# The low half of every third MLP weight chunk by an adding DMA, in a one-core hybrid decoder step

## The chip, the cores and the metric

The kernel runs on one core of a Trainium2 chip. The metric is the time of one execution on the device, in microseconds. The engines that appear below are TensorE (PE; its weight loads are listed as PEld), VectorE (DVE), ScalarE (ACT), GpSimd (POOL) and SyncE (SP), and the DMA queues that SP, ACT and POOL issue to.

## The reference

One layer of a hybrid decoder trunk is computed for 256 prompt tokens and 8 sample tokens, 264 columns in all, with a width of 2048. Three gated branches (pooling, a gated linear recurrence, a Conformer convolution) are merged and projected, and a squared-ReLU MLP follows. Everything is float32. Cut to what matters here:

```python
x = x + (g_a * y_pool + g_b * y_lru + g_c * y_conf) @ w_out
hid = jnp.square(jax.nn.relu(rms_norm(x, g_mlp) @ w_up))   # w_up   (2048, 8192)
x = x + hid @ w_down                                       # w_down (8192, 2048)
...
y_prompt = rms_norm(xp, g_final)
```

## The kernel before, in words

Activations are kept transposed, features on the 128 partitions and the 264 tokens along the row. TensorE multiplies in the rounded format float32r, and a float32 product is made of three: both operands are written as a high half (the value rounded) plus a low half (the value less its rounding), and `mm3` (lines 183 to 187) adds high times high (L185), high times low (L186) and low times high (L187) into one accumulator.

All weights come as one stream. `weight_plan` cuts it into groups, and each group into chunks of 128 rows by 1024 numbers (512 KB); a chunk of a dense group holds two blocks of 128 input rows by 512 output columns, and so feeds 2 x 4 x 3 = 24 products. The order of the groups in the MLP is, for each quarter q of the 8192 hidden features: four groups of the up projection, `("w_up", 0, 16, q*4+m)`, then four of the down projection, `("w_down", q*16, 16, m)`, eight chunks each. So a quarter is 64 chunks, and the two halves of a quarter 32 each.

A chunk passes through three buffers. SP's DMA brings chunks in pairs (1 MB, `dma_pair`, L138) into `raw`, which has six slots. `split` (lines 156 to 163) makes its two halves: ACT casts the raw chunk to the high half in `whi` (L162), and DVE subtracts that from the raw chunk into `wlo` (L163). `whi` and `wlo` have four slots each. Then PE multiplies.

The order of every engine's work is the order of the calls, written out by hand in one loop over the chunks. In step i of the loop come, in this order: the split of chunk i+3; in even steps, the DMA of chunks i+8 and i+9; the products of chunk i; after the last chunk of a group, what takes its four accumulators away; and the background work that falls due, taken from small queues by a budget for each engine. The waits between engines follow from the buffers: the split of chunk i+3 writes the slots of `whi` and `wlo` that chunk i-1 used, and the DMA of chunks i+8 and i+9 writes the slots of `raw` that chunks i+2 and i+3 used.

For a tile of the up projection the accumulator is clipped and scaled by DVE (L806), squared and cast by ACT (L810, L811), and its low half taken by DVE (L815), a step or two later. For a tile of the down projection DVE adds the accumulator to the residual (L830), and in the last quarter ACT squares it and POOL sums the squares (L796). Otherwise POOL has no work in the MLP, and it issues no DMA anywhere in the kernel. The program sets aside 1024 bytes of each partition for descriptors of POOL's DMAs (`dynamic_dma_scratch_size=1024`).

Of the kernel before, what the change touches and what calls it, by code (L numbers as in the profile page):

```python
# [12 lines left out]
AF = mybir.ActivationFunctionType  # L13
ALU = mybir.AluOpType
# [37 lines left out]
EARLY = 2  # L52
WIDE = 4
ROW = N + CH


def weight_plan():

    groups = [("w_lru_in", 0, 2 * WIDE, 0)] + [("w_in", WIDE, KD - WIDE, m) for m in (1, 2)]
    groups += [("w_in", 0, 16, m) for m in (0, 3, 4, 6, 5)]
    for g in range(4):
        groups += [("w_gate", 0, 16, t) for t in ((0, 4, 1), (5,), (2, 6), (3, 7))[g]]
        groups += [("w_pool_br", 0, 4, g), ("w_lru_br", 0, 8, g)]
    groups += [("w_gate", 0, 16, 8 + g) for g in range(3)]
    groups += [("w_conf_br", 0, 4, 0), ("w_gate", 0, 16, 11)]
    groups += [("w_conf_br", 0, 4, g) for g in range(1, 4)]
    groups += [("w_out", 0, 16, m) for m in range(4)]
    for q in range(4):  # L70
        groups += [("w_up", 0, 16, q * 4 + m) for m in range(4)]
        groups += [("w_down", q * 16, 16, m) for m in range(4)]
    chunks = []
    for gi, (name, _, k, m) in enumerate(groups):
        for c in range(k // 2):
            chunks.append(("wide" if name == "w_lru_in" else "dense", gi, c, CH))
            if name == "w_in" and (m, c) in LRU_AT:
                chunks.append(("lru", LRU_AT.index((m, c)), 0, 512))
            if (name, m) == ("w_gate", 0) and c == 3:
                chunks += [("grp", 0, 0, 512), ("none", 0, 0, 0)]  # L80
    return groups, chunks
# [3 lines left out]
def hybrid_step(ctx: ExitStack, tc: tile.TileContext, head_in, x_in, par_in, st_in, wall, y_out, st_out):  # L85
    nc = tc.nc
# [4 lines left out]
    def f(ap):  # L91
        return ap.bitcast(F32)
# [5 lines left out]
    qtmp = cpool.tile([P, 16 * N], F32, name="qtmp", tag="Q")  # L98
    first = cpool.tile([P, KD + EARLY * ROW], F32, name="first")
    early = first[:, KD:].rearrange("p (k c) -> p k c", k=EARLY)  # L100
# [29 lines left out]
    groups, chunks = weight_plan()  # L130
# [25 lines left out]
    def split(j, a=0, b=CH):  # L156
        if j >= len(chunks) or not chunks[j][3]:
            return
        h, lo = whi[:, j % NHI, :], wlo[:, j % NHI, :]
        s = slice(a, min(b, chunks[j][3]))  # L160
        r = early[:, j, N + s.start:N + s.stop] if j < EARLY else raw[:, j % NRAW, s]
        nc.scalar.copy(h[:, s], r)  # L162
        nc.vector.tensor_tensor(lo[:, s], r, f(h[:, s]), op=ALU.subtract)  # L163

    def sent(x):
# [125 lines left out]

    cuts = [0, KD + N + 256, KD + ROW, KD + ROW + N + 512, KD + 2 * ROW]
    for a, b in zip(cuts, cuts[1:]):
# [614 lines left out]
    for a in range(0, CH, 256):  # L908
        split(0, a, a + 256)
    for c in (1, 2):  # L910
        x_tile(c)
        split(c, 0, 512)
        split(c, 512, CH)
# [198 lines left out]
```

## Time and profile before

| | |
|---|---|
| measured time, median of two runs | 1300.28 us (1300.14 to 1300.42) |
| span of the profiled execution, first to last instruction | 1299.3 us |
| TensorE busy | 1287.7 us, 99% of the span |
| DVE busy | 834.7 us, 64% |
| ACT busy | 717.7 us, 55% |
| POOL busy | 104.6 us, 8% |
| moved by DMA | 256.96 MB, 198 GB/s over the span |
| share of the 16 DMA engines' time, SP's queue | 57.8% |

The profiled execution's own span stands 1.0 us below the median of the measured runs. Busy times are sums over one execution. An engine's row in a list of groups gives the line, the operation, what it writes and reads, the count, the total and the mean, and then how long the engine sat idle just before these instructions and what ended that. Rows in order of time begin with the start, in microseconds from the first instruction, and the length. A row of 40 numbers cuts its window into 40 equal slices.

### The profile page before, as it was taken

The numbers are of one execution on the slowest core, as the hardware profiler recorded it, in microseconds if no ns is written. First come the engines' busy times: TensorE is split into PE (matmuls) and PEld (weight loads), VectorE is DVE, ScalarE is ACT, GpSimd is POOL, SyncE is SP. The second block draws the span as 40 slices with busy tenths as digits, with TensorE's granted clock in tenths as the row PEclk, the third lists the DMA queues.
The fourth block names the chain that finished last, engine by engine and source line by source line (L and its number), as shares of the span: only waits on it lengthen the run. The fifth ranks groups of instructions, "written<-read, shape, count | busy, mean of one in ns | idle before, by whom it ended". The sixth has DMA issues, their size and how long they took to land.

```text
span 1299.3 us, 26672 instructions
## 1 busy us (share of the span) xinstructions
PE 1287.7 (99%) x11434; PEld 1286.8 (99%) x11434; DVE 834.7 (64%) x1058; ACT 717.7 (55%) x1021; POOL 104.6 (8%) x124
## 2 busy tenths in 40 slices
PE   9999999999999999999999999999999999999996
PEld 9999999999999999999999999999999999999996
DVE  6896898776776677666655555655555555555554
ACT  7767677667674655455544334543344533354543
POOL 0250010110102023021000000000000000000013
PEclk9999999999999999999999999999999999999998
DMA  8656566555565564656555555555555555555551
GB/s 337 220 186 202 191 207 200 195 195 198 196 229 193 186 206 161 232 185 206 195 194 198 195 197 194 198 197 194 197 195 196 195 197 195 197 196 196 195 195 68
DMA packets 38711, 256.96 MB, mean 198 GB/s; under 512 B 4288, under 2 KB 5312, under 8 KB 9152
## 3 DMA queue, kind: packets, MB, share of 16 engines
q1 hardware_dynamic: 38304, 254.78, 57.8%
q8 instruction: 89, 1.46, 0.4%
q10 hardware_dynamic: 288, 0.47, 0.1%
q14 instruction: 30, 0.25, 0.1%
HBM read 252.03 MB, written 3.21 MB: 196 GB/s over the span
## 4 chain that ended last, share of the span: by engine, by line
PE 99%; DVE 0%; DMA 0%; ACT 0%; SPq 0%; DVEq 0%; issue 0%
PE acc L187 33%; PE acc L186 33%; PE acc L185 33%; PE acc L894 1%; DMA first<-head_dram 0%; DVE raw L999 0%; PE acc L980 0%; SPq L151 0%; DVE acc L993 0%; DVEq L1091 0%; DVE G L992 0%; DVE G L991 0%; ACT whi L162 0%; ACT A L284 0%; PE acc L259 0%
## 5 line engine op out<-in xcount | busy, mean ns | idle before, releaser
L163 DVE TENSOR_TENSOR wlo<-raw,whi 128x1024 fp32r<-128x1024 f32 (+1 forms) x479 | 585.6, 1225 | 442.1 <-ACT whi L162 436.5
L162 ACT CAST whi<-raw 128x1024 fp32r<-128x1024 f32 (+1 forms) x479 | 493.6, 1033 | 526.1 <-PE acc L186 474.7
L187 PE MATMUL acc<-A,wlo 128*128 128x264 f32 x1952 | 538.9, 276 | 0.0
L186 PE MATMUL acc<-A,whi 128*128 128x264 f32 x1952 | 538.8, 276 | 0.0
L185 PE MATMUL acc<-A,whi 128*128 128x264 f32 x1952 | 538.7, 276 | 0.0
L187 PEld LDWEIGHTS acc<-A,wlo 128*128 128x128 f32 x1952 | 368.9, 189 | 0.1
L185 PEld LDWEIGHTS acc<-A,whi 128*128 128x128 f32 x1952 | 368.9, 189 | 0.0
L186 PEld LDWEIGHTS acc<-A,whi 128*128 128x128 f32 x1952 | 368.9, 189 | 0.0
L186 PE MATMUL acc<-xn,whi 128*128 128x264 f32 x1024 | 282.6, 276 | 0.0
L187 PE MATMUL acc<-xn,wlo 128*128 128x264 f32 x1024 | 282.6, 276 | 0.0
L185 PE MATMUL acc<-xn,whi 128*128 128x264 f32 x1024 | 282.6, 276 | 0.0
L185 PEld LDWEIGHTS acc<-xn,whi 128*128 128x128 f32 x1024 | 193.5, 189 | 0.0
L186 PEld LDWEIGHTS acc<-xn,whi 128*128 128x128 f32 x1024 | 193.5, 189 | 0.0
L187 PEld LDWEIGHTS acc<-xn,wlo 128*128 128x128 f32 x1024 | 193.5, 189 | 0.0
L186 PE MATMUL acc<-Q,whi 128*128 128x264 f32 x644 | 177.7, 276 | 0.0
L185 PE MATMUL acc<-LH,whi 128*128 128x264 f32 x640 | 176.6, 276 | 0.0
L187 PE MATMUL acc<-LH,wlo 128*128 128x264 f32 x640 | 176.6, 276 | 0.0
L186 PEld LDWEIGHTS acc<-Q,whi 128*128 128x128 f32 x644 | 121.7, 189 | 0.0
L185 PEld LDWEIGHTS acc<-LH,whi 128*128 128x128 f32 x640 | 121.0, 189 | 0.0
L187 PEld LDWEIGHTS acc<-LH,wlo 128*128 128x128 f32 x640 | 121.0, 189 | 0.0
L796 POOL TENSOR_TENSOR G<-G 128x264 f32<-128x264 f32 x28 | 25.5, 911 | 745.3 <-ACT G L794 744.4
L576 ACT ACTIVATE G<-tmp,par 128x256 f32<-128x256 f32 x120 | 54.2, 499 | 2.9 <-DVE G L579 2.0
(186 smaller groups left out, 797.3 us busy)
## 6 DMA issues: line engine op xcount, KB each, us to landing
raw<-wall_dram SPq DMA_DIRECT2D x230, 1024.0 KB, 4.9
raw<-wall_dram SPq DMA_DIRECT2D x10, 512.0 KB, 7.0
raw<-wall_dram SPq DMA_DIRECT2D x5, 256.0 KB, 3.0
X<-x_dram SPq DMA_DIRECT2D x4, 264.0 KB, 8.5
so_dram<-st SPq DMA_DIRECT2D x1, 1018.0 KB, 9.1
st<-st_dram SPq DMA_DIRECT2D x1, 912.0 KB, 9.8
y_dram<-raw SPq DMA_DIRECT2D x4, 198.0 KB, 2.2
X<-x_dram SPq DMA_DIRECT2D x1, 528.0 KB, 9.9
```

The costliest lines, as they stand in the source:

```text
L162: nc.scalar.copy(h[:, s], r)
L163: nc.vector.tensor_tensor(lo[:, s], r, f(h[:, s]), op=ALU.subtract)
L185: nc.tensor.matmul(ps[:, :N], whi_t, xh, start=first, stop=False)
L186: nc.tensor.matmul(ps[:, :N], whi_t, xl, start=False, stop=False)
L187: nc.tensor.matmul(ps[:, :N], wlo_t, xh, start=False, stop=last)
L576: nc.scalar.activation(dst[:, ct, :TP], vext[:, ct, k:k + TP], AF.Copy, scale=par[:, w:w + 1])
L796: nc.gpsimd.tensor_tensor(sq2, sq2, t, op=ALU.add)
L894: nc.tensor.matmul(pair[m][:, :N], w[:, m * P:(m + 1) * P], sent(A[:, x, :]), start=start and k == 0, stop=False)
```

## The change

For chunks of the up projection and of two of the four quarters of the down projection (the second and third, whose first rows are blocks 16 and 32), and of those only the chunks whose index in the stream divides by three, the low half is made in another way. ACT, after its cast, writes the negated rounding of the raw chunk to the low half's slot. POOL then issues a DMA from `raw` to that slot which adds what it brings to what stands there. The value is the same: minus the rounding, plus the raw weight. DVE's subtraction is not issued for these chunks. Of the stream's 478 chunks 192 are in the named groups (indices 222 to 253 and 286 to 445), and 64 of these divide by three.

```diff
+LOW_BY_DMA = (("w_up", 0), ("w_down", 16), ("w_down", 32))
...
         nc.scalar.copy(h[:, s], r)
+        if chunks[j][0] == "dense" and groups[chunks[j][1]][:2] in LOW_BY_DMA and j % 3 == 0:
+            nc.scalar.activation(lo[:, s], r, AF.Copy, scale=-1.0)
+            nc.gpsimd.dma_start(lo[:, s], r, accum_op=ALU.add)
+            return
         nc.vector.tensor_tensor(lo[:, s], r, f(h[:, s]), op=ALU.subtract)
```

## The prediction

> **What bounds the kernel now.** I read the page first (busy shares, then the chain that ended last), then the busy time of the stretches that the change touches, then one period of the weight pipeline in order of time, and last the DMA rows. The page:
>
> ```profile
> span 1299.3 us, 26672 instructions
> PE 1287.7 (99%) x11434; PEld 1286.8 (99%) x11434; DVE 834.7 (64%) x1058; ACT 717.7 (55%) x1021; POOL 104.6 (8%) x124
> PE 99%; DVE 0%; DMA 0%; ACT 0%; SPq 0%; DVEq 0%; issue 0%
> ```
>
> TensorE is the whole chain. The up and down projections fill the last 690 us; by the plan's order the groups that the diff names lie in two stretches, the up projection of the first quarter (595.8 to 682.2) and then everything from the second up projection to the fourth (768.6 to 1200.6). In these two and the one between them:
>
> ```profile
> core 0: us, PE busy (x) PEld busy (x) DVE busy (x) ACT busy (x) POOL busy (x), PEclk, DMA share, GB/s
> 595.80:682.20 86.40, 86.40 (x770) 86.40 (x769) 53.28 (x71) 47.91 (x69) 3.31 (x4) 1.00 0.58 194
> 682.20:768.60 86.40, 86.40 (x770) 86.40 (x769) 46.04 (x53) 36.41 (x40) 0.00 (x0) 1.00 0.59 196
> 768.60:1200.60 432.00, 432.00 (x3842) 432.00 (x3841) 238.47 (x285) 199.77 (x248) 0.00 (x0) 1.00 0.58 195
> ```
>
> PE is busy for every microsecond of them at full clock. DVE stands at 55% and ACT at 46% of the long stretch, so work taken from DVE there buys no time: **the best this change can do is nothing**. The stretches hold 32 and 160 chunks, 2.70 us each (432.00/160); every index divisible by three makes 64 chunks (43 of the up, 21 of the down projection). The question is only whether the new low half comes in time. One period, in order of time:
>
> ```profile
> 819.75 0.33 SPq L138 DMA_DIRECT2D raw<-wall_dram  x1
> ...
> 820.03 0.28 PE L185 MATMUL acc<-xn,whi 128*128 128x264 f32 x1
> ...
> 820.12 1.04 ACT L162 CAST whi<-raw 128x1024 fp32r<-128x1024 f32 x1 [1.65 <-PE acc L186]
> ...
> 820.15 0.19 PEld L187 LDWEIGHTS acc<-xn,wlo 128*128 128x128 f32 x1
> ```
>
> ```profile
> 821.20 1.23 DVE L163 TENSOR_TENSOR wlo<-raw,whi 128x1024 fp32r<-128x1024 f32 x1 [0.78 <-ACT whi L162]
> ...
> 822.73 0.28 PE L185 MATMUL acc<-xn,whi 128*128 128x264 f32 x1
> ...
> 828.13 0.28 PE L185 MATMUL acc<-xn,whi 128*128 128x264 f32 x1
> ...
> 828.25 0.19 PEld L187 LDWEIGHTS acc<-xn,wlo 128*128 128x128 f32 x1
> ```
>
> At 820.03 PE starts step i. That frees the buffer of chunk i-1, and with four buffers this is the one for chunk i+3. ACT's cast starts 0.09 later, released by PE; DVE writes the low half until 822.43. PE starts step i+3 three periods later, at 828.13, and loads its first low weights at 828.25. Counted from the step's start, the low half is there at 2.40 and wanted at 8.22: today 5.8 us lie idle in between. **That slack is all the change has to live on.**
>
> **What is removed.** 64 of DVE's subtractions, 64 x 1.226 = 78.5 us of DVE time:
>
> ```profile
> L163 DVE TENSOR_TENSOR wlo<-raw,whi 128x1024 fp32r<-128x1024 f32 x160 | 196.2, 1226 | 193.5 <-ACT whi L162 191.2
> L162 ACT CAST whi<-raw 128x1024 fp32r<-128x1024 f32 x160 | 167.3, 1046 | 230.8 <-PE acc L186 228.3
> ```
>
> DVE waits for ACT in front of nearly every one of them. Worth on the path: 0.
>
> **What is added on ACT.** A second pass over the chunk (the negated rounding), same shape and engine as the cast: 64 x 1.046 = 66.9 us. It follows the cast at once, so the next thing of ACT is 1.05 us later in one step of three. ACT idles 1.65 us ahead of its casts, which covers it; only beside the squares of the up projection (about two steps in eight) is ACT full, and there the next cast is late by at most that 1.05 us, with 5.8 us of slack behind it. Cost 0. The new pass ends at 0.09 + 2 x 1.08 = 2.25 after the step's start (1.08 is from the cast's start, 820.12, to what it releases, 821.20).
>
> **What is added on POOL.** 64 DMAs, each from raw into the low half, adding. They wait for ACT. Behind them on POOL stands nothing: the long stretch has 0.00 us of POOL work, and only its last quarter's sums of squares come later. From 2.25 the transfer has 5.97 us to land.
>
> **What the transfer costs.** No POOL DMA and no adding one is in the trace. The nearest rows are the weight loads of twice its size, one of them in a window of 6 us (its 40 slices are 0.15 us each), and the stores of y at the end (a window from 1287, slices of 0.325 us):
>
> ```profile
> L138 SPq DMA_DIRECT2D raw<-wall_dram x124: 327/328/328, 599.6 to 1262.6; - x124
> DMA to landing us min/median/max: 4.6/4.9/5.8
> ```
>
> ```profile
> DMA  0000000000000098702268799979797979724000
> raw<-wall_dram SPq DMA_DIRECT2D x1, 1024.0 KB, 4.8
> ```
>
> ```profile
> 771.15 16.53 SPq L138 DMA_DIRECT2D raw<-wall_dram  x4
> ```
>
> ```profile
> GB/s 0 0 0 0 0 0 0 0 0 0 0 0 0 175 385 375 366 336 336 406 380 392 240 377 357 397 383 395 380 445 408 122 24 0 0 0 0 0 0 0
> y_dram<-raw SPq DMA_DIRECT2D x2, 264.0 KB, 2.8
> ```
>
> The load issued at 771.15 has its first bytes moving at about 772.1 (0.95 us), its last at 775.5, and has landed at 775.95 (0.45). Its engine time is the share: 0.58 x 5.40 us a pair = 3.13 us for 1 MB. Stores that leave SBUF run near 385 GB/s, 2.7 us for 1 MB. The adding transfer writes 0.5 MB and reads 1 MB (raw, and the low half itself). **Lower end**, as if it were a plain copy of 0.5 MB: 1.57 us of engine time. **Upper end**: there is no row for the adder's rate; I bound it by twice the 2.7 us of 1 MB, 5.4. I take 2.7, both operands counted at the rate of the row that leaves SBUF, since that is the nearest in kind. For POOL's own part, SP's issue of 0.33 us is the lower bound; I take 0.74, the shortest of POOL's passes over a 128x264 tile:
>
> ```profile
> L796 POOL TENSOR_TENSOR G<-G x28: 742/756/1403, 532.7 to 1285.7; 128x264 f32<-128x264 f32 x28
> ```
>
> Alone, it lands at 2.25 + 0.74 + 0.95 + 2.7 + 0.45 = 7.09, in time by 1.1 us.
>
> The Trainium skill, "Collectives: The Full Stack", on why ReduceScatter is half of AllGather, says that a reducing DMA is slow because of its two source reads on one queue, not because of the adder; no run shown here can tell. By that rule the sum is the one with 2.7, without it the lower end.
>
> **But it isn't alone.** raw has six slots, refilled two at a time by SP, and SP now has to wait for the adding DMA to have read its slot. Today SP issues a pair each 5.4 us, at 2.42 into a step (819.75 against 817.33, the start of the step before 820.03), as DVE releases it:
>
> ```profile
> SPq L138 <- DVE wlo L163: 473.5, 95, 6.4
> ```
>
> Take the six steps from the start of step 6m as 0. The refill behind chunks 6m+2 and 6m+3 waits for the add of chunk 6m+3, 7.1 to 8.1; the refill behind it, whose own release comes at 2 x 2.70 + 2.42 = 7.8, queues right after. So 2 MB of loads go out together at about 7.9, moving from 8.85 to 8.85 + 6.26 = 15.1. The next add (chunk 6m+6) is ready at 8.10 + 2.25 = 10.35 and moving at 10.35 + 0.74 + 0.95 = 12.04, with 3.1 us of loads still to go. If the two share the engines evenly, its 2.7 us take 5.4: moved at 17.44, landed at 17.9. It is wanted at 16.20 + 0.12 = 16.32: **1.6 us late**, and PE stands for it. The third refill goes out only then, so the add after that one (moving 3.9 us after its step starts) meets a load almost finished, and is in time. One add in two is late: 32 x 1.6 = 51 us. The refills themselves are in time: a pair issued at 8.2 and held up to about 16 is first cast at 5 x 2.70 + 0.09 = 13.59 at the earliest for one chunk, and that chunk has the 5.8 us of slack.
>
> **Sum.** Span 1299.3 + 51 = 1350.3. The two measured runs have a median of 1300.28, 1.0 above the span, so 1351. With the add's engine time between 2.2 and 3.4 the lateness goes from 0.6 to 2.7 (at 3.4 the load ends first), so this case runs from 1319 to 1387.
>
> **The rivals.** *All hidden.* The point from which it decides is an add that lands within 5.97 us of its start beside a load in flight. With 1.57 us of engine time and 0.33 of issue it moves from 11.63 to 14.8 and has landed at 15.2, ahead of 16.32: no stall, PE as before, 1300. For it: 42% of the DMA time is idle. Against it: the loads come in bunches, and the second operand has to be read. The Trainium skill, "DMA: Bandwidth & Descriptors", on the anatomy of a DMA issued by GpSimd, gives 2.0 us plus the bytes over 436 GB/s; for 1 MB that is an estimate of 4.4 us, in time here with 1.6 to spare; the load's row, 4.9, is a little above that rule.
>
> *The adder is slow.* At 5.4 us of engine time an add that meets no load lands at 9.8, already 1.6 late, each time: 64 x 1.6 = 102. And six chunks need 9.4 us of loads and 10.8 of adds, 20.2 in 16.2 us: DMA becomes the bound, 32 x 4.0 = 128. With the bunching on top I put it at 150: 1450. It decides from 3.83 us of engine time (5.97 less 0.74, 0.95 and 0.45). For it: an operation of which no row says anything. Against: nothing in the trace.
>
> *Faster.* Only through the end, where the time after PE's last product is DVE's; the diff leaves the last down projection as it is. I give it 0.01.
>
> **How the numbers follow.** One add in two late 0.46, all hidden 0.31, slow adder 0.22, faster 0.01. The predicted time is that of the first, 1351. The range goes from 1299 (hidden) to 1460, which takes in the upper end of the unknown rate and leaves out the worse half of the slow adder; the likeliest case's own range is 1319 to 1387. Two per cent, 26 us, is about what a measurement of this kernel can tell from no change: it is 0.8 us for each late add. Below it lie the hidden case and a tenth of the first: 0.35. Slower: 0.42 + 0.22 = 0.64. Faster: 0.01.
>
> **What would show it.** Right: PE's busy time about 1288 still in a longer span, with idle ahead of products or weight loads of L187 put down to the DMA into wlo, 1 to 3 us, about 30 times, in both stretches and nowhere else; two weight loads landing late (over 6 us) out of every three; L163 at 415 instead of 479; the adding DMA landing near 5 us and near 7.5 us in turn. Wrong: stalls at all 64 (then the rate or POOL's part is the larger term), no idle of PE at all, stalls on the cast of ACT (then the refills of raw are what is late), or a granted clock below 1.00 in these stretches, which today's rows have nowhere there.

## The result, and the profile after

The changed kernel takes 1396.67 us (median of two runs, 1391.26 and 1402.08) against 1300.28: a ratio of 1.074, with a 95% interval of 1.064 to 1.084. It is 96 us slower. The profiled execution has a span of 1389.5 us, 90.2 above the one before, and the numbers below are worked out against that. Five lines are new, so the loads' line 138 has become L139, ACT's cast in line 162 is L163, DVE's subtraction in line 163 is L168, and L185 to L187 are L190 to L192.

The head of the page, its chain, and the groups that are new or changed:

```profile
span 1389.5 us, 26849 instructions
PE 1322.3 (95%) x11434; PEld 1315.6 (95%) x11434; DVE 756.7 (54%) x994; ACT 778.2 (56%) x1085; POOL 160.4 (12%) x188
q0 software_dynamic: 9216, 33.56, 13.0%
PE 81%; DMA 13%; ACT 4%; issue 1%; DVE 1%; DVEq 0%
L168 DVE TENSOR_TENSOR wlo<-raw,whi 128x1024 fp32r<-128x1024 f32 (+1 forms) x415 | 507.1, 1224 | 590.6 <-ACT whi L163 586.9
L166 POOL DMA_DIRECT2D wlo<-raw x64 | 55.7, 871 | 636.5 <-ACT wlo L165 549.7
L165 ACT ACTIVATE wlo<-raw 128x1024 fp32r<-128x1024 f32 x64 | 67.3, 1052 | 0.0
```

DVE lost 78.0 us of work, ACT gained a pass of 67.3, and neither moved the end (a run further down has ACT's pass alone). What did is in the chain: 13% of it is now the adding DMA. The table of waits says how often PE stood for it (total, times, longest), and the answer on line 166 how long the adds took to land:

```profile
PEld acc L192 <- DMA wlo<-raw: 61.7, 30, 4.1
```

```profile
L166 POOL DMA_DIRECT2D wlo<-raw x64: 859/869/1024, 589.3 to 1279.3; - x64
DMA to landing us min/median/max: 4.5/6.7/10.3
```

30 of 64 adds were late, by 2.06 us on the mean. That is 61.7 us, and 28.5 of the 90.2 are left. POOL's own issue took 0.86 to 1.02 us for all 64 adds, late or not, so the lateness does not arise there. PE is *busier* than before by 34.6 us with the same 11434 products. Two stretches right after one of the waits, and the chain across it (start, length, what), show why:

```profile
core 0: us, PE busy (x) PEld busy (x) DVE busy (x) ACT busy (x) POOL busy (x), PEclk, DMA share, GB/s
905.10:908.50 3.40, 3.40 (x18) 3.40 (x17) 0.00 (x0) 0.57 (x1) 0.00 (x0) 0.50 0.76 220
909.00:913.00 4.00, 4.00 (x38) 4.00 (x37) 3.52 (x6) 1.04 (x1) 0.00 (x0) 1.00 0.68 153
```

```profile
895.46 8.44 DMA wlo<-raw
903.95 0.38 PE acc L192
...
905.42 0.22 PE acc L190
905.64 0.22 PE acc L191
905.86 0.22 PE acc L192
...
908.69 0.11 PE acc L190
908.81 0.11 PE acc L191
```

The add landed at 903.9, and about a microsecond later the granted clock fell to 0.50 for 3.4 us: products 0.22 us apart instead of 0.11. The waits divide in two. 15 lasted 2.39 us or more, 48.3 us together, and each of them was followed by such a slow stretch; 15 lasted 1.96 us or less, and none of them was. The 15 stretches at 0.50 are 58.0 us long (13 of 3.41 us, two of 6.83), so half of that, 29 us of work, was lost in them. That is the 28.5 that the waits leave. The row of the whole part of the program with adds agrees: 0.04 of 680 us is 27, where before the change the clock stood at 1.00.

```profile
600.00:1280.00 680.00, 624.22 (x5244) 618.46 (x5242) 253.85 (x333) 334.79 (x407) 54.85 (x64) 0.96 0.76 218
```

So a long wait is paid twice, once as idle time and once as slow products after it; a short one is paid once.

Why an add is late shows in one of them. SP issued two loads in the 0.80 us from 913.40, the second at 913.82, and POOL the add at 916.09. Here are those issues, and who used the DMA engines in the 4.5 us after the add's issue and in the 4 us after that (queue, packets, MB, share of the engines):

```profile
913.40 0.80 SPq L139 DMA_DIRECT2D raw<-wall_dram  x2
```

```profile
916.09 0.86 POOL L166 DMA_DIRECT2D wlo<-raw  x1 [11.67 <-ACT wlo L165]
```

```profile
q1 hardware_dynamic: 194, 1.46, 97.5%
```

```profile
q0 software_dynamic: 144, 0.52, 66.2%
q1 hardware_dynamic: 31, 0.12, 8.7%
```

From 916.1 to 920.6 the engines moved nothing but loads. Then all 144 packets of the add moved within 4 us. It did not share the engines evenly with the loads in front of it: it stood behind them. All 15 of the long waits have this picture, two loads issued together, 0.4 to 3.5 us ahead of the add.

### The profile page after: what moved, and what is told of

The parts are those of the page before. It is cut to its first block, busy times and chain, and to the rows that moved or that the text cites. A ratio compares the mean times of both kernels' runs of the same rounds, so it can differ in the third digit from the quotient of the medians.

```text
span 1389.5 us, 26849 instructions
## 1 busy us (share of the span) xinstructions
PE 1322.3 (95%) x11434; PEld 1315.6 (95%) x11434; DVE 756.7 (54%) x994; ACT 778.2 (56%) x1085; POOL 160.4 (12%) x188
## 3 DMA queue, kind: packets, MB, share of 16 engines
q0 software_dynamic: 9216, 33.56, 13.0%
## 4 chain that ended last, share of the span: by engine, by line
PE 81%; DMA 13%; ACT 4%; issue 1%; DVE 1%; DVEq 0%
PE acc L192 27%; PE acc L191 26%; PE acc L190 26%; DMA wlo<-raw 13%; ACT whi L163 2%; ACT wlo L165 2%; PE acc L899 1%; DVE raw L1004 0%; PE acc L306 0%; DVE wlo L168 0%; ACT xn L782 0%; ACT G L799 0%; PE acc L985 0%; DVE xn L787 0%; DVE acc L998 0%
## 5 line engine op out<-in xcount | busy, mean ns | idle before, releaser
L168 DVE TENSOR_TENSOR wlo<-raw,whi 128x1024 fp32r<-128x1024 f32 (+1 forms) x415 | 507.1, 1224 | 590.6 <-ACT whi L163 586.9
L163 ACT CAST whi<-raw 128x1024 fp32r<-128x1024 f32 (+1 forms) x479 | 493.4, 1033 | 555.7 <-PE acc L191 475.4
L192 PE MATMUL acc<-A,wlo 128*128 128x264 f32 x1952 | 540.8, 277 | 8.8 <-DMA wlo<-raw 8.8
L190 PE MATMUL acc<-A,whi 128*128 128x264 f32 x1952 | 540.3, 277 | 0.0
L192 PEld LDWEIGHTS acc<-A,wlo 128*128 128x128 f32 x1952 | 370.5, 190 | 9.8 <-DMA wlo<-raw 9.8
L190 PEld LDWEIGHTS acc<-A,whi 128*128 128x128 f32 x1952 | 370.5, 190 | 0.0
L192 PE MATMUL acc<-xn,wlo 128*128 128x264 f32 x1024 | 292.9, 286 | 36.3 <-DMA wlo<-raw 36.1
L190 PE MATMUL acc<-xn,whi 128*128 128x264 f32 x1024 | 290.2, 283 | 0.0
L191 PE MATMUL acc<-xn,whi 128*128 128x264 f32 x1024 | 290.1, 283 | 0.0
L192 PEld LDWEIGHTS acc<-xn,wlo 128*128 128x128 f32 x1024 | 201.1, 196 | 40.5 <-DMA wlo<-raw 40.4
L190 PEld LDWEIGHTS acc<-xn,whi 128*128 128x128 f32 x1024 | 201.0, 196 | 0.0
L191 PEld LDWEIGHTS acc<-xn,whi 128*128 128x128 f32 x1024 | 200.9, 196 | 0.0
L192 PE MATMUL acc<-LH,wlo 128*128 128x264 f32 x640 | 180.2, 282 | 10.7 <-DMA wlo<-raw 10.7
L190 PE MATMUL acc<-LH,whi 128*128 128x264 f32 x640 | 179.7, 281 | 0.0
L192 PEld LDWEIGHTS acc<-LH,wlo 128*128 128x128 f32 x640 | 123.9, 194 | 11.5 <-DMA wlo<-raw 11.5
L166 POOL DMA_DIRECT2D wlo<-raw x64 | 55.7, 871 | 636.5 <-ACT wlo L165 549.7
L190 PEld LDWEIGHTS acc<-LH,whi 128*128 128x128 f32 x640 | 124.0, 194 | 0.0
L165 ACT ACTIVATE wlo<-raw 128x1024 fp32r<-128x1024 f32 x64 | 67.3, 1052 | 0.0
```

Of the source, the lines that this page charges most:

```text
L165: nc.scalar.activation(lo[:, s], r, AF.Copy, scale=-1.0)
L166: nc.gpsimd.dma_start(lo[:, s], r, accum_op=ALU.add)
L190: nc.tensor.matmul(ps[:, :N], whi_t, xh, start=first, stop=False)
L191: nc.tensor.matmul(ps[:, :N], whi_t, xl, start=False, stop=False)
L192: nc.tensor.matmul(ps[:, :N], wlo_t, xh, start=False, stop=last)
```

## The experiments

Times below are medians; the kernel before ran on the same chips at 1300.7 to 1300.9. Theory A, from the prediction: adds are late because refills of `raw`, held back by the add before them, go out in pairs and stand in front. Theory B: every add has a price of its own. Theory C: loads and adds meet anyway, held back or not.

**One add in six chunks.** `j % 3 == 0` becomes `j % 6 == 0`.

> Every sixth chunk instead of every third: 32 adds, one in 16.2 us. Theory A (an add is late only when two refills of raw, held back by the add before, stand in front of it): no add is late, 1300 to 1305, every add landing near 4.5 to 5 us, clock 1.00 throughout. Rival B (each add costs PE something by itself, by its latency and POOL's part): half of the loss stays, near 1345.

Measured 1301.42, ratio 1.0007 (0.9998 to 1.0017).

```profile
PEld acc L192 <- DMA wlo<-raw: 1.2, 5, 0.3
```

An add without another one in the six chunks is in time, and costs nothing; B falls. 64 adds cost 96 us, and half of them none.

**The constant block.** The add brings other data of the same size, so nothing holds the refills.

```diff
-            nc.gpsimd.dma_start(lo[:, s], r, accum_op=ALU.add)
+            nc.gpsimd.dma_start(lo[:, s], early[:, 0, N:], accum_op=ALU.add)
```

> The 64 adds bring a constant block (chunk 0's raw weights) instead of the raw chunk, so the refill of raw no longer waits for them; the low halves are then other numbers, the traffic is the same. Theory A, if the held refills are the whole cause: loads go out every 5.4 us again, no add is late, 1300 to 1310. Rival C (adds and loads meet anyway, since in every second add a load is released in the same step): one add in two late by 1.3 to 4 us, 1345 to 1450.

Measured 1448.02, ratio 1.1136 (1.1120 to 1.1153): *slower* than the change by 51 us. The waits of PE, and an add's issue beside the load's:

```profile
PEld acc L192 <- DMA wlo<-first: 91.5, 31, 4.8
```

```profile
1007.07 0.33 SPq L139 DMA_DIRECT2D raw<-wall_dram  x1
```

```profile
1007.45 0.86 POOL L166 DMA_DIRECT2D wlo<-first  x1 [11.56 <-ACT wlo L165]
```

So A falls as the whole cause. Without the tie, the load is released by the same pass of ACT that releases the add, goes out 0.4 us ahead of it, and the add stands behind it: 31 late adds of 2.95 us. The tie had kept at least the add's own refill behind it. This is C, in a sharper form, theory D: **an add waits for every load issued ahead of it, and is late where one went out just before.** "Ahead" counts from the add's first packet, which in the run with one add in six comes 1.4 us after POOL starts its issue, at the soonest. In the change a load issued at 903.96, 0.4 us *after* an add's issue at 903.56, still moved from 904.5 on, and the add only from 907.5.

**The phase.** D says that where the adds fall against the loads decides, with the same traffic. Loads go out in even steps. Indices 0 and 2 modulo six put the splits of all adds into odd steps; 0 and 3 put every second one into an even step. The number of adds in six chunks stays two.

```diff
-... and j % 3 == 0:
+... and j % 6 in (0, 2):
```

With the constant block:

> A constant block is added, as before, so no refill waits for an add; but the adds fall on chunks whose index modulo six is 0 or 2, the same two in six, where before it was 0 and 3. Their splits are then all in odd steps, and loads go out in even ones. Theory D (an add waits for every load issued ahead of it, and is late only where one went out just before): each add is ready at 3.7 us after its step's start, when the load of the step before has just moved; it lands at 6.9 to 7.4 us, ahead of 8.2: 1300 to 1310. Rival (the DMA engines are simply too full with this traffic): about 1448 again.

Measured 1318.15, ratio 1.0139 (1.0116 to 1.0161).

```profile
PEld acc L192 <- DMA wlo<-first: 16.1, 10, 5.0
```

130 us faster than the constant block at 0 and 3, with the same loads and as many adds: the DMA engines are not too full. In 51 of the 54 adds that were in time the nearest load was issued 2.0 to 3.7 us ahead. It is not the 1300 to 1310 that was expected: ten waits are left. Three of them, of 3.6 to 5.0 us, make 12.7 of the 16.1, and D covers one of these three, with a load issued 0.3 us ahead. Before the other two the load went out 2.78 us ahead, as it did for dozens of adds that were in time. In one of them, issued at 959.72, most of the add had moved by 964.5, but its last packets came one by one until 969, beside a load that was issued 2.6 us *behind* it (the two windows are 961 to 964.5 and 964.5 to 969.7):

```profile
q0 software_dynamic: 130, 0.48, 69.5%
q1 hardware_dynamic: 64, 0.40, 37.2%
```

```profile
q1 hardware_dynamic: 135, 0.97, 56.0%
q0 software_dynamic: 14, 0.05, 4.8%
```

So D is not the whole rule: now and then an add's tail is overtaken by a later load. Why is open.

With the raw chunk, so that refills wait again:

> The raw chunk is added, as in the change, for indices 0 and 2 modulo six. The refills wait for the adds again and so move towards the next one: by theory D the second add of each six is some 0.5 us late, 1310 to 1340. If holding the refills is harmless, 1300 to 1305; if the phase doesn't matter, about 1396.

Measured 1402.58, ratio 1.0761 (1.0720 to 1.0803), near the change itself.

```profile
PEld acc L192 <- DMA wlo<-raw: 73.2, 32, 4.4
```

The forecast by D had the sign right and the size wrong: 2.3 us late and not 0.5, and then the clock. The time is rather that of the rival beside it, that the phase doesn't matter (1396). The trace is against that rival, and so is the pair of runs with the constant block: 27 of the 32 late adds here have one load issued within 1.3 us of their own issue (up to 0.6 us after it), where the long waits of the change had two, issued together further ahead. Refills that wait have shifted, so that loads and adds meet again. The four runs together:

| | refills wait for the add | refills free |
|---|---|---|
| indices 0 and 3 of six | 1396.7 (the change) | 1448.0 |
| indices 0 and 2 of six | 1402.6 | 1318.2 |

Neither the phase alone nor the tie alone makes the loss. Three combinations put a load in front of about one add in two (30, 31 and 32 of 64 were late); the fourth doesn't (10).

**A copy in place of the add.** `accum_op=ALU.add` is left out.

> The 64 DMAs of POOL copy raw to the low half and don't add (the low halves are then wrong by that). If the second operand's read is what fills the DMA engines, their time goes from 2.7 us to about 1.4 each, and by my queue of loads and adds none is late: 1300 to 1310. If POOL's part and the waiting behind the loads is what counts, and not the size, the copies land as late as the adds and the loss stays above 60.

Measured 1335.87, ratio 1.0244 (1.0192 to 1.0297). The rows below are of an execution of 1321.28, the least of the four; the other three took 1336 to 1337, so the rows account for 20 of the 35 us, and where the rest goes isn't shown.

```profile
q0 software_dynamic: 9216, 33.56, 7.0%
```

```profile
PEld acc L192 <- DMA wlo<-raw: 17.2, 19, 2.7
```

The page counts the same 33.56 MB, but the engines' time is 7.0% of a span of 1319.5, 1.44 us a transfer, against 13.0% of 1389.5, 2.82 us, for the add. So the adding transfer takes twice the engine time of the copy, as the Trainium skill, "Collectives: The Full Stack", on why ReduceScatter is half of AllGather, has it of a reduce with two source reads; the trace agrees. Both expectations missed: half the size took away two thirds of the loss, not all and not none. A transfer half as long still stands behind the loads: ahead of 18 of these 19 waits stand two loads, issued within 2.0 to 4.1 us before the copy.

**The adds to one side.** They go to a block nobody reads; DVE makes the low half.

```diff
             nc.scalar.activation(lo[:, s], r, AF.Copy, scale=-1.0)
-            nc.gpsimd.dma_start(lo[:, s], r, accum_op=ALU.add)
-            return
+            nc.gpsimd.dma_start(early[:, j % 2, N:], r, accum_op=ALU.add)
```

> The 64 adds go to a block that nobody reads, and DVE makes the low half as before (after ACT's pass). The refills of raw still wait for the adds. Theory A: PE waits for nothing, though loads go out in bunches and some land late: 1300 to 1305. Rival: late refills of raw hold up ACT's casts and cost by themselves, 1310 to 1340.

Measured 1300.83, ratio 1.0000 (0.9991 to 1.0010). The traffic, and refills held by the adds, cost nothing. Only PE's wait for the low half does.

**ACT's pass alone.** The same without any DMA of POOL.

> ACT's negated pass alone, 64 times, and then DVE's subtraction over it as before; no DMA of POOL. Prediction's step: ACT's time is covered, 1300 to 1302. Rival: ACT's 1.05 us in one step of three delays casts where ACT is full, up to 1310.

Measured 1300.97, ratio 1.0001 (0.9992 to 1.0010). The pass is covered.

**As many adds, spread out.** `j % 4 == 0` over all up and down projections.

> 64 adds again, but every fourth chunk, over all up and down projections. Theory A: an add lands before the two refills behind it meet the next add, six chunks' bunch doesn't build up: 1300 to 1310, clock 1.00. Rival B (a price for each add): the same 64 adds cost the same, about 1390.

Measured 1314.79, ratio 1.0109 (1.0072 to 1.0147).

```profile
PEld acc L192 <- DMA wlo<-raw: 12.1, 19, 2.1
```

64 adds for 14 us instead of 96, so B is out once more; it is a little above the 1300 to 1310 that was expected, so the spacing isn't quite enough. No wait is over 2.1 us here, and the clock of this run is 0.997, as before the change.

**Waits of a known length.** One add in six, which has no wait of its own, with one or two passes of POOL ahead of it.

```diff
+            nc.gpsimd.tensor_tensor(early[:, 1, N:], lo[:, s].bitcast(F32), early[:, 0, N:], op=ALU.mult)
+            nc.gpsimd.tensor_tensor(early[:, 1, N:], early[:, 0, N:], early[:, 1, N:], op=ALU.mult)   # second kernel alone
             nc.gpsimd.dma_start(lo[:, s], r, accum_op=ALU.add)
```

> Every sixth chunk (32 adds, no bunches), and POOL does one pass of about 3 us over a block ahead of each add, so that each lands near 10.0 us after its step's start, 1.8 us late. Without a price of the clock: 32 x 1.8 = 58, near 1358. If waits under 2 us keep the clock at full speed, the same; if every wait lowers it, 32 x 1.7 more, near 1410.

> As the kernel with one pass of POOL, but two passes, 6 us: each add 4.9 us late. Waits alone: 32 x 4.9 = 157, near 1457. If each wait over some 2 us also halves the granted clock for one stretch of 3.4 us, 1.7 us more each: 211, near 1511.

Measured 1350.79, ratio 1.0381 (1.0360 to 1.0401), and 1514.49, ratio 1.1642 (1.1625 to 1.1659). The waits of the first, then of the second, and two stretches after one of the second's waits, which ended at 839.8:

```profile
PEld acc L193 <- DMA wlo<-raw: 45.8, 33, 2.7
```

```profile
PEld acc L194 <- DMA wlo<-raw: 136.9, 33, 4.5
```

```profile
core 0: us, PE busy (x) PEld busy (x) DVE busy (x) ACT busy (x) POOL busy (x), PEclk, DMA share, GB/s
839.00:844.00 5.00, 4.21 (x23) 4.21 (x24) 0.00 (x0) 0.00 (x0) 0.00 (x0) 0.66 0.68 235
844.00:857.00 13.00, 13.00 (x118) 13.00 (x117) 6.77 (x8) 7.66 (x10) 5.36 (x2) 1.00 0.42 156
```

The passes were shorter than estimated, so the waits are 1.39 and 4.15 us on the mean. The first kernel's span is 1350.5: 51.2 over before, of which 45.8 are waits, so 0.16 us a wait is left for the clock. The second's is 1513.8: 214.5 over, 136.9 waits, and 2.35 us a wait on top; the mean clock is 0.66 just after a wait and 1.00 later. The long waits are paid one and a half times over, the short ones about once. That the second is near the 1511 of its forecast is luck: the waits were shorter than the 4.9 us assumed, and the clock's price was higher than the 1.7, because 21 of the 33 slow stretches lasted 6.83 us and not 3.41.

## Why the prediction was right or wrong

The forecast of 1351, in a range of 1299 to 1460, had the sign and the place, and about half of the size: 51 us forecast, 96 measured. The time lies above the 1319 to 1387 that was given for this case alone; it is within the whole range only because that range reached up to a slow adder, which wasn't there. That is luck, and not the mechanism. Step by step:

- *Worth on the path: 0; ACT's pass: 0.* Right: one add in six takes 33 passes from DVE and gains nothing, 1.0007; ACT's pass alone gives 1.0001.
- *The add's own time.* Right: 2.82 us of engine time against 2.7 taken, 0.87 us on POOL against 0.74, and 4.5 us to landing where no load was in the way against 4.84 by the sum. The slow adder is out.
- *One add in two is late, because loads stand ahead of it.* Right in number: 30 waits against 32, in both stretches. The number is partly luck: 15 of them lasted 0.2 to 2.0 us and 15 lasted 2.4 to 4.1, so the loss sits in one add in four.
- *1.6 us late each.* **This term was too small**: 2.06. It was worked out with both queues sharing the engines evenly; for 4.5 us the engines gave 97.5% of their time to the loads that were first, and nothing to the add. The steady pattern drawn for it was too regular as well: landings ran from 4.5 to 10.3 us, where 5 and 7.5 in turn were foretold.
- *The price of a wait is its length.* **This is the step that failed.** The sum had no term for the granted clock, though a clock below 1.00 stood in its list of signs against it. It is worth 28.5 us, a third of the loss, as what the waits leave of the 90.2, and 29 by the length of the slow stretches.
- *Why loads stand ahead.* Half right. The tie between refill and add was named as the cause, and the pairs of loads that it foretold stand ahead of all 15 long waits. But the tie isn't needed for the loss: the constant block shows that this phase collides without it, and worse.
- *Refills of `raw` are in time.* Right for what it was used for: with the adds to one side, nothing is lost. The sign given for it, two loads of three over 6 us, was wrong: loads between 790 and 1270 us landed in 5.4 us at the median, up to 10.4.
- *All hidden.* With 1.44 us of engine time, nearly the lower end, the copy still costs 35 us, so the second operand alone didn't decide this rival; the place in the queue did. The estimate of 4.4 us that the prediction made by the Trainium skill, "DMA: Bandwidth & Descriptors", on the anatomy of a DMA issued by GpSimd, fits an add that meets no load, 4.5, and says nothing of one that does.

## What to carry to other kernels

An engine off the critical path gives no time when it is relieved; what counts is the slack of the thing handed over, here 5.8 us. A transfer that must land within such a slack has to be costed with the whole queue in front of it, not by its own length and not by a mean share of the engines: look at what is issued in the microseconds ahead of it, and shift its phase. And a wait of TensorE over about 2 us mostly cost more than its length here, because the clock fell after it.

## What the runs showed of the hardware that was not expected

- A wait of TensorE of 2.7 us, counted on its weight loads as all waits here (up to 903.9, above), was followed by 3.4 us at a granted clock of 0.50; a kernel whose longest wait was 2.1 us kept 0.997, and one with 33 waits of 4.15 us fell to 0.937. Over all the runs with late transfers here, none of 105 waits up to 2.07 us was followed by a slow stretch, and 101 of 107 from 2.14 us up were; the longest that wasn't is 3.35 us, so the border is not sharp. The Trainium skill, "TensorE: Matmul & The Clock Gate", part 1, puts the half clock after an idle window of about 3.4 us, and the full clock after a busy one of that length. The half and the 3.4 us of slow work agree; that a shorter wait suffices is what these traces show.
- A POOL transfer issued 2.3 us after the second of two loads of SP's queue moved nothing for 4.5 us, then all of its 0.52 MB; without loads in the way its first packet moves after 1.4 us. The Trainium skill, "DMA: Bandwidth & Descriptors", on arbitration (in its section on queues, rings and completion order), has each engine drain a whole packet, typically 9 to 17 descriptors, from one queue before it takes up another. The two loads are 288 packets of the trace, 9 an engine for each load; whether 9 of them make one packet in that sense the trace doesn't tell, so it neither confirms this rule nor speaks against it.
- An adding transfer takes twice the engine time of a copy of its size, 2.82 against 1.44 us a transfer for 512 KB.
